# First down-projection weights in the up-projection's buffers, and another order of the loads at the turn

## The chip, the core and the metric

The kernel runs on one core of a Trainium2 chip. The metric is the device time of one execution in microseconds (us). The core has five engines that run side by side, each through its own list of instructions in order: PE (matrix products; PEld is its weight load), DVE and ACT (elementwise work), POOL, and SP, which here does nothing but issue DMA transfers. An engine that waits for one instruction holds up all that stand behind it in its list.

## The reference, cut to what matters

Two layers, 1024 tokens of 1024 channels. Each has a token mixer and then this channel mixer, about which the change is:

```python
x = layer_norm(ALPHA * x + mixed, ln1_g[l], ln1_b[l])
ff = jnp.square(jax.nn.relu(x @ w_up[l])) @ w_down[l]
x = layer_norm(ALPHA * x + ff, ln2_g[l], ln2_b[l])
```

## The kernel before

Both products of the channel mixer are done by a seven-product scheme for 2x2 blocks (Strassen's, in Winograd's form), and each float32 operand is split into a high and a low part, so that one product is three matmuls (high x high, high x low, low x high). ACT makes the high part (L97) and DVE the low one (L100).

**Up.** The hidden columns are taken in 16 pairs. A pair's weights are turned into seven forms; forms 3 to 7 stand in the tag `y4` of the pool `big` (8 buffers of 4 KB a partition). Each form is multiplied with one of seven forms of x (`x11`, `x21`, `x22`, `xt1` in the tag `b16` of `big`, the others in the up pool). Sums are in PSUM (`uz`, `uc`, `ud`); DVE and ACT make hidden parts from them (`h`), DVE the four further combinations that the down product needs (`hs`), and SP stores them to DRAM (`hd`).

**Down.** Two groups `gr` of hidden rows, in each seven products in the order 3, 1, 5, 6, 2, 7, 4, and in each product four quarters q of 24 matmuls: 96 matmuls a product. For a quarter, `down_raw` loads 2 MB of down weights (`wd`, four transfers of 512 KB) into the `b16` buffers, each as its form of x is done with; `down_forms` splits them (`wf`), loads the fitting hidden parts back (`hr`, two transfers of 256 KB) and splits these (`hf`). The sums (`db`, and `dz` for the products 1, 6, 7) are added to eight rows `yd`, loaded from DRAM into the `y4` buffers, 512 KB each. `l2g` and `l2b` are scales of the last norm, 512 KB each as written out over the partitions.

**The turn.** The pool `pd` of the down stage takes the place of the up stage's pool `pu`. A `wf` buffer can be written only when all that stood at its place is done with, the stores of `h` and `hs` to DRAM among it.

The program is written in order, and a scheduler then moves instructions past each other on each engine. All transfers named here are issued by SP, on one queue; transfer n waits for the landing of transfer n minus 8. The lines at the turn:

```python
for t in range(NTB):
    ys[t] = ytile(f"yd{l}_{t}")
for q in range(NQ):
    down_raw(0, q)
for t in range(NTB):
    nc.sync.dma_start(ys[t], xmid[l][t])
g = bcast(ln2_g[l], D, pd, "g", f"l2g{l}")
b = bcast(ln2_b[l], D, pd, "b", f"l2b{l}")
...
steps = [(gr, i) for gr in range(2) for i in PRODS]
cur = [down_forms(0, PRODS[0], q) for q in range(NQ)]
```

Of the kernel before, what the change touches and what calls it, by code (L numbers as in the profile page):

```python
# [12 lines left out]
F32R = mybir.dt.float32r  # L13
# [39 lines left out]
def encoder(ctx: ExitStack, tc: tile.TileContext, x, memt, w_f, w_v, w_mk, w_mv, w_out, w_up,  # L53
# [680 lines left out]
    for l in range(L):  # L734
# [230 lines left out]
        with ExitStack() as es:  # L965
# [18 lines left out]
            def down_forms(gr, i, q):  # L984

                r = wr[gr, q]
                v = {k: r[:, :, k[0], k[1]] for k in ((0, 0), (0, 1), (1, 0), (1, 1))}
                tt = nc.vector.tensor_tensor
                if i == 5:
                    tt(v[0, 0], v[0, 1], v[0, 0], op=ALU.subtract)  # L990
                    tt(v[0, 1], v[1, 1], v[0, 1], op=ALU.subtract)
                elif i == 6:
                    tt(v[1, 1], v[1, 1], v[0, 0], op=ALU.subtract)
                elif i == 4:
                    tt(v[1, 0], v[1, 1], v[1, 0], op=ALU.subtract)
                w = pd.tile([P, 2, 2, 512], F32R, tag="wf", name=f"wf{l}_{gr}_{i}_{q}", bufs=4)
                split(w[:, 0], w[:, 1], v[place[i]])
                hr = wts.tile([P, 2, 512], F32, tag="raw", name=f"hr{l}_{gr}_{i}_{q}", bufs=3)
                p0 = 2 * (NQ * gr + q)
                for n in range(2):  # L1000
                    loads.append(nc.sync.dma_start(hr[:, n], hd[p0 + n][:, form_of[i]]))
                if gr and i == PRODS[-1]:
                    if q % 2 == 0:
                        wr["h", q // 2] = pd.tile([P, 2, 2, 2, 512], F32R, tag="wd", name=f"hl{l}_{q}", bufs=2)
                    h = wr["h", q // 2][:, q % 2]
                else:
                    h = wts.tile([P, 2, 2, 512], F32R, tag="w8", name=f"hf{l}_{gr}_{i}_{q}", bufs=3)
                split(h[:, 0], h[:, 1], hr)
                return w, h

            for t in range(NTB):
                ys[t] = ytile(f"yd{l}_{t}")
            for q in range(NQ):
                down_raw(0, q)
            for t in range(NTB):
                nc.sync.dma_start(ys[t], xmid[l][t])
            g = bcast(ln2_g[l], D, pd, "g", f"l2g{l}")
            b = bcast(ln2_b[l], D, pd, "b", f"l2b{l}")
            touched = set()

            def add(t, j, ps, op=ALU.add):
# [24 lines left out]
            def down(ps, fm, t, start, stop):  # L1046
                w, h = fm
                ts = slice(t * P, t * P + P)
                for n in range(2):
                    for m, (a, c) in enumerate(((0, 0), (0, 1), (1, 0))):  # L1050
                        nc.tensor.matmul(ps, lhsT=h[:, a, n, ts], rhs=w[:, c, n], start=start and n == 0 and m == 0,  # L1051
                                         stop=stop and n == 1 and m == 2, skip_group_check=True)

            def done(t, spread, parts=1):
# [4 lines left out]
                    nc.sync.dma_start(dst[:, cs], ys[t][:, cs])  # L1059

            steps = [(gr, i) for gr in range(2) for i in PRODS]
            cur = [down_forms(0, PRODS[0], q) for q in range(NQ)]
            late = []
            for n, (gr, i) in enumerate(steps):
                if i in (1, 6, 7):
                    if i == 1:
                        z = banks(gr, f"dz{l}_{gr}")
                    ps = z
                else:
                    ps = banks(1 - gr, f"db{l}_{gr}_{i}")  # L1070
                nxt = []
                final = n == len(steps) - 1
                if n == 2:
                    for q in range(2):
                        down_raw(1, q)
                if final:
                    if not last:
                        first = proj_w(l + 1, FIRST)
                        xn = new_xt(f"x{l + 1}")
                    for t in range(4):  # L1080
                        for q in range(NQ):
                            down(ps[t], cur[q], t, q == 0, q == NQ - 1)
                        evict(i, t, ps[t])
                        done(t + 4, {1: 1}.get(t, 0), 2 if last and t == 3 else 1)
                        if not last:
                            to_xt(ys[t], xn, t, f"l2_{l}_{t}")
                    break
                for q in range(NQ):
                    for t in range(4):
                        down(ps[t], cur[q], t, q == 0 and i not in (6, 7), q == NQ - 1 and i not in (1, 6))  # L1090
                    if q == NQ - 1:
                        for t in range(4):
                            evict(i, t, ps[t])
                            if gr and i == 2:
                                done(t, {1: 1, 3: 1}.get(t, 0))
                    nxt.append(down_forms(*steps[n + 1], q))
                    if not gr and i == PRODS[-2] and q > 1:
                        down_raw(1, q)
                cur = nxt
# [90 lines left out]
```

## Time and profile before

| what | us |
|---|---|
| median of 3 runs | 2515.94 (2515.7 to 2519.42) |
| the profiled execution's own time | 2514.72 |
| its span, first to last instruction | 2512.9 |
| PE busy | 2335.6 |
| DVE busy | 1894.5 |
| ACT busy | 1105.5 |

The profile is of one execution. It holds each instruction's start and length by engine, what ended each idle time, the clock granted to PE as a share of full speed, and for each DMA its issue and its landing.

### The profile page before, as it was taken

What the parts mean: (1) busy time and instruction counts of PE and PEld (TensorE: products, weight loads), DVE (VectorE), ACT (ScalarE), POOL (GpSimd) and SP (SyncE); (2) the same over time, 40 slices, a digit from 0 to 9 for tenths busy, and PEclk for the clock granted to TensorE, in tenths of its full rate; (3) what the DMA queues carried; (4) which work ended last, traced back from release to release, by engine and by line L of the source; (5) the groups of instructions that cost most, each with busy time, mean ns of one, the idle gap of its engine ahead of it and who ended that gap; (6) DMA issues with size and microseconds to landing.
All of it is one profiled execution on the core that took longest, in us unless ns stands there. A gap on an engine that the chain in (4) does not pass through costs nothing.

```text
span 2512.9 us, 30298 instructions
## 1 busy us (share of the span) xinstructions
PE 2335.6 (93%) x11256; PEld 1919.2 (76%) x11256; DVE 1894.5 (75%) x2598; ACT 1105.5 (44%) x1864; POOL 486.3 (19%) x350
## 2 busy tenths in 40 slices
PE   5999989889999997999999999889989999799997
PEld 3788777677788886888878887767768888588886
DVE  7599779969756656657788977997885666476769
ACT  5212477722555543333431237874245555333332
POOL 1124176821000000000033324683100000000002
PEclk9999999999999998999999999998989999899998
DMA  9433444242344458243332336422424444934332
GB/s 317 154 125 97 152 131 127 67 147 90 114 161 148 151 213 326 92 163 98 107 109 84 116 120 187 123 69 87 168 76 153 149 155 148 385 101 159 99 92 101
DMA packets 137740, 355.74 MB, mean 142 GB/s; under 512 B 14804, under 2 KB 31956, under 8 KB 130900
## 3 DMA queue, kind: packets, MB, share of 16 engines
q1 hardware_dynamic: 137592, 353.81, 42.1%
q8 instruction: 88, 1.44, 0.3%
q14 instruction: 60, 0.49, 0.1%
HBM read 240.47 MB, written 117.47 MB: 142 GB/s over the span
## 4 chain that ended last, share of the span: by engine, by line
PE 59%; DVE 20%; issue 3%; DMA 3%; ACT 1%; SPq 0%; DVEq 0%; ACTq 0%
PE uz L873 13%; PE db L1051 12%; PE dz L1051 10%; PE uc L873 7%; PE ud L873 4%; DVE acc L344 3%; DVE s L535 3%; DVE s L557 2%; PE wo_ps L115 1%; PE wo_ps L114 1%; PE wo_ps L113 1%; DVE l_row L145 1%; PE pj L114 1%; PE pj L113 1%; PE pj L115 1%
## 5 line engine op out<-in xcount | busy, mean ns | idle before, releaser
L1051 PE MATMUL db<-wf,hf 128*128 128x512 f32 x1344 | 324.9, 403 | 22.2 <-ACT wf L97 18.6
L1051 PEld LDWEIGHTS db<-wf,hf 128*128 128x128 f32 x1344 | 258.9, 193 | 87.0 <-ACT wf L97 20.8
L163 POOL TENSOR_TENSOR yd<-yd,l2g 128x1024 f32<-128x1024 f32 x6 | 14.7, 2443 | 1345.5 <-ACT yd L162 1345.5
L1051 PE MATMUL dz<-wf,hf 128*128 128x512 f32 x1152 | 269.7, 395 | 0.0
L97 ACT ACTIVATE hf<-hr 128x1024 fp32r<-128x1024 f32 x104 | 110.3, 1061 | 353.7 <-PE db L1051 195.1
L1051 PEld LDWEIGHTS dz<-wf,hf 128*128 128x128 f32 x1152 | 217.0, 188 | 50.7
L100 DVE TENSOR_TENSOR hf<-hr,hf 128x1024 fp32r<-128x1024 f32 x104 | 127.2, 1223 | 152.4 <-ACT hf L97 152.0
L97 ACT ACTIVATE wu<-wu_r 128x512 fp32r<-128x512 f32 (+1 forms) x192 | 131.0, 699 | 227.7 <-PE uc L873 95.5
L873 PE MATMUL uz<-xt,wu 128*128 128x512 f32 x768 | 190.5, 396 | 6.0 <-ACT wu L97 6.0
L873 PE MATMUL uz<-x,wu 128*128 128x512 f32 x768 | 191.6, 396 | 0.0
L344 DVE SCALAR_TENSOR_TENSOR acc<-u,pp,acc 128x1009 f32<-128x1009 f32 (+14 forms) x120 | 182.3, 1560 | 0.6
L114 PE MATMUL pj<-x_l,wf 128*128 128x512 f32 x448 | 177.3, 396 | 2.7 <-DVE x_l L100 2.7
L113 PE MATMUL pj<-x_h,wf 128*128 128x512 f32 x448 | 178.2, 398 | 0.4 <-ACT x_h L97 0.4
L115 PE MATMUL pj<-x_h,wf 128*128 128x512 f32 x448 | 176.5, 395 | 0.0
L100 DVE TENSOR_TENSOR wu<-wu_r,wu 128x512 fp32r<-128x512 f32 (+1 forms) x192 | 145.7, 777 | 39.6 <-ACT wu L97 39.2
L873 PEld LDWEIGHTS uz<-xt,wu 128*128 128x128 f32 x768 | 144.3, 188 | 40.3 <-ACT wu L97 6.5
L537 ACT ACTIVATE s<-s,ast 128x1024 f32<-128x1024 f32 x128 | 147.2, 1151 | 55.2 <-DVE ast L535 52.9
L873 PEld LDWEIGHTS uz<-x,wu 128*128 128x128 f32 x768 | 146.4, 191 | 32.0
L890 DVE TENSOR_TENSOR h<-u,uc 128x512 f32<-128x512 f32 x64 | 44.0, 688 | 160.4 <-PE uc L873 134.2
L535 DVE CUSTOM_DVE_ANT_0 s<-sc,bt 128x1024 f32<-128x1024 f32 x128 | 153.8, 1214 | 11.6 <-PE sc L533 10.1
L100 DVE TENSOR_TENSOR wf<-wd,wf 128x1024 fp32r<-128x1024 f32 x112 | 138.1, 1236 | 26.4 <-DMA l2b<-in_ln_b 13.4
L97 ACT ACTIVATE wf<-wd 128x1024 fp32r<-128x1024 f32 x112 | 116.6, 1045 | 35.7 <-DMA hd<-hs 30.2
(261 smaller groups left out, 5375.7 us busy)
## 6 DMA issues: line engine op xcount, KB each, us to landing
hr<-hd SPq DMA_DIRECT2D x224, 256.0 KB, 2.9
wu_r<-in_w_up SPq DMA_DIRECT2D x64, 512.0 KB, 4.2
hd<-hs SPq DMA_DIRECT2D x128, 256.0 KB, 2.3
wd<-in_w_down SPq DMA_DIRECT2D x64, 512.0 KB, 7.6
hd<-h SPq DMA_DIRECT2D x96, 256.0 KB, 2.2
ks<-kd SPq DMA_DIRECT2D x32, 512.0 KB, 11.6
wf_raw<-in_w_f SPq DMA_DIRECT2D x28, 512.0 KB, 4.2
qd<-stg SPq DMA_DIRECT2D x8, 1024.0 KB, 4.2
```

What stands on the lines that cost most here:

```text
L97: nc.scalar.activation(hi, src, AF.Copy)
L100: (lo_eng or nc.vector).tensor_tensor(lo, src, f(hi), op=ALU.subtract)
L113: nc.tensor.matmul(ps, lhsT=lhs[0], rhs=rhs[0], start=start, stop=False)
L114: nc.tensor.matmul(ps, lhsT=lhs[0], rhs=rhs[1], start=False, stop=False)
L115: nc.tensor.matmul(ps, lhsT=lhs[1], rhs=rhs[0], start=False, stop=stop)
L344: nc.vector.scalar_tensor_tensor(acc[:, c, a:b], u[:, c, a + t - PAD:b + t - PAD], pp[:, k:k + 1], acc[:, c, a:b], ALU.mult, ALU.add)
L535: nc.vector.tensor_tensor_reduce(out=sc[:, m], in0=ps.rearrange("p a b -> p (a b)"), in1=bt[:, b0:b0 + T], scale=-0.125, scalar=3e38, op0= ...
L537: nc.scalar.activation(sc[:, m], sc[:, m], AF.Exp, scale=-1.0, bias=st[:, m:m + 1], accum_out=st[:, 2 + m:3 + m])
L557: nc.vector.scalar_tensor_tensor(sc[:, 0], sc[:, 1], st[:, 5:6], sc[:, 0], ALU.mult, ALU.add)
L873: nc.tensor.matmul(ps, lhsT=a[:, kc], rhs=x[:, c, kc], start=start and kc == 0 and n == 0, stop=stop and kc == 3 and n == 2, skip_group_ch ...
L890: nc.vector.tensor_tensor(h, a, ps, op=op)
L1051: nc.tensor.matmul(ps, lhsT=h[:, a, n, ts], rhs=w[:, c, n], start=start and n == 0 and m == 0, stop=stop and n == 1 and m == 2, skip_group ...
```

## The change

The first product's weight parts for q = 0 and 1 no longer take two `wf` buffers of `pd`. They take four `y4` buffers, the high and the low part each its own tile. Raw weights and forms of a quarter are written one after the other, not all raw weights first. The rows `yd` are loaded in two lots: four after q = 1, and four with the second product, into the buffers that the first weight parts leave. The norm scales are loaded with the third product, behind the raw weights of group 1.

```diff
-                w = pd.tile([P, 2, 2, 512], F32R, tag="wf", name=f"wf{l}_{gr}_{i}_{q}", bufs=4)
-                split(w[:, 0], w[:, 1], v[place[i]])
+                if not gr and i == PRODS[0] and q < 2:
+
+                    w = [big.tile([P, 2, 512], F32R, tag="y4", name=f"wf{l}_{gr}_{i}_{q}_{n}", bufs=8) for n in range(2)]
+                else:
+                    w = pd.tile([P, 2, 2, 512], F32R, tag="wf", name=f"wf{l}_{gr}_{i}_{q}", bufs=4)
+                    w = [w[:, 0], w[:, 1]]
+                split(w[0], w[1], v[place[i]])
...
-            for t in range(NTB):
-                ys[t] = ytile(f"yd{l}_{t}")
-            for q in range(NQ):
-                down_raw(0, q)
-            for t in range(NTB):
-                nc.sync.dma_start(ys[t], xmid[l][t])
-            g = bcast(ln2_g[l], D, pd, "g", f"l2g{l}")
-            b = bcast(ln2_b[l], D, pd, "b", f"l2b{l}")
+            def down_rows(ts):
+                for t in ts:
+                    ys[t] = ytile(f"yd{l}_{t}")
+                    nc.sync.dma_start(ys[t], xmid[l][t])
+
...
-                        nc.tensor.matmul(ps, lhsT=h[:, a, n, ts], rhs=w[:, c, n], start=start and n == 0 and m == 0,
+                        nc.tensor.matmul(ps, lhsT=h[:, a, n, ts], rhs=w[c][:, n], start=start and n == 0 and m == 0,
...
-            cur = [down_forms(0, PRODS[0], q) for q in range(NQ)]
+            cur = []
+            for q in range(NQ):
+                down_raw(0, q)
+                cur.append(down_forms(0, PRODS[0], q))
+                if q == 1:
+                    down_rows(range(4))
...
+                if n == 1:
+                    down_rows(range(4, NTB))
                 if n == 2:
                     for q in range(2):
                         down_raw(1, q)
+                    g = bcast(ln2_g[l], D, pd, "g", f"l2g{l}")
+                    b = bcast(ln2_b[l], D, pd, "b", f"l2b{l}")
```

What the scheduler makes of it differs from before only at the two turns from up to down, one in each layer, in the same way. On PE this stood at the turn of the first layer before (`uz_15`, `uc_15`: the last pair's sums; `db_0_3_t`: first product, token block t; `wf_0_3_q`, `hf_0_3_q`: weights and hidden parts of quarter q):

```order
L873 MATMUL uc_14_7534<-x_0_4994,wu_14_3_7381 128x512 x12
L873 MATMUL uz_15_7483<-xt_0_5338,wu_15_7_7528 128x512 x12
L873 MATMUL uc_15_7626<-x_0_4994,wu_15_3_7531 128x512 x12
L1051 MATMUL db_0_3_0_7798<-wf_0_3_0_7762,hf_0_3_0_7768 128x512
L1051 MATMUL db_0_3_1_7799<-wf_0_3_0_7762,hf_0_3_0_7768 128x512
```

and this stands there now, of which each block of `db` matmuls is shown by its first row:

```order
L873 MATMUL uc_14_7534<-x_0_4994,wu_14_3_7381 128x512 x12
L1053 MATMUL db_0_3_0_7788<-wf_0_3_0_0_7727,hf_0_3_0_7734 128x512
...
L873 MATMUL uz_15_7483<-xt_0_5338,wu_15_7_7528 128x512 x12
L1053 MATMUL db_0_3_0_7788<-wf_0_3_1_0_7742,hf_0_3_1_7749 128x512
...
L1053 MATMUL db_0_3_1_7789<-wf_0_3_0_0_7727,hf_0_3_0_7734 128x512
...
L873 MATMUL uc_15_7626<-x_0_4994,wu_15_3_7531 128x512 x12
L1053 MATMUL db_0_3_2_7790<-wf_0_3_0_0_7727,hf_0_3_0_7734 128x512
...
L1053 MATMUL db_0_3_0_7788<-wf_0_3_2_7765,hf_0_3_2_7771 128x512
L1053 MATMUL db_0_3_1_7789<-wf_0_3_2_7765,hf_0_3_2_7771 128x512
```

Matmuls of the down product now stand between the last three blocks of the up product: 6 before `uz_15`, 18 between it and `uc_15` (6 of block 0, 12 of block 1), and 24 behind it (blocks 2 and 3), before those of q = 2.

On SP the queue stood so before, from the third quarter's raw weights (`wd_0_2`) to the last store of a hidden combination but one (`hs_15_1`):

```order
L981 DMA wd_0_2_7740<-in_w_down 128x1024 x4
L1016 DMA yd_2_7724<-xmid_101 128x1024
...
L1016 DMA yd_3_7725<-xmid_101 128x1024
L1016 DMA yd_4_7726<-xmid_101 128x1024
L1016 DMA yd_5_7727<-xmid_101 128x1024
L1016 DMA yd_6_7728<-xmid_101 128x1024
...
L981 DMA wd_0_3_7745<-in_w_down 128x1024 x4
L1016 DMA yd_7_7729<-xmid_101 128x1024
L896 DMA hd_15_5209<-hs_15_2_7708 128x512
L896 DMA hd_15_5209<-hs_15_0_7706 128x512
L896 DMA hd_15_5209<-hs_15_1_7707 128x512
```

and so now:

```order
L981 DMA wd_0_2_7760<-in_w_down 128x1024 x4
...
L1019 DMA yd_0_7752<-xmid_101 128x1024
L1019 DMA yd_1_7754<-xmid_101 128x1024
L1019 DMA yd_2_7756<-xmid_101 128x1024
...
L1019 DMA yd_3_7758<-xmid_101 128x1024
L981 DMA wd_0_3_7774<-in_w_down 128x1024 x4
L896 DMA hd_15_5209<-hs_15_2_7708 128x512
L896 DMA hd_15_5209<-hs_15_0_7706 128x512
L1019 DMA yd_4_7930<-xmid_101 128x1024
L896 DMA hd_15_5209<-hs_15_1_7707 128x512
```

Four rows fewer stand ahead of `wd_0_3`, and `yd_4`, which takes a buffer of the first weight parts, now stands ahead of the store of `hs_15_1`.

On ACT the four weight parts followed the last hidden part (`h_15_3`) before; now those of q = 0 and 1 stand further up, the first of them ahead of `h_15_0`, and behind `h_15_3` stand two hidden parts and then the weights of q = 2 and 3 (DVE has the low parts in the same order):

```order
L892 ACTIVATE h_15_3_7702<-h_15_3_7702 128x512
L97 ACTIVATE hf_0_3_3_7785<-hr_0_3_3_7782 128x1024
L97 ACTIVATE hf_0_1_0_7822<-hr_0_1_0_7819 128x1024
L97 ACTIVATE wf_0_3_2_7765<-wd_0_2_7760 128x1024
L97 ACTIVATE wf_0_3_3_7779<-wd_0_3_7774 128x1024
L97 ACTIVATE wf_0_1_0_7816<-wd_0_0_7722 128x1024
```

`hf_0_3_3` and `hf_0_1_0` take the buffers of `hf_0_3_0` and `hf_0_3_1`, so they wait until PE has used these for all four token blocks. At its place in `pd`, `wf_0_3_3` now waits for the store of `hs_15_1`, as `wf_0_3_1` did before.

## Rows read from the trace of the kernel before

**Rows 1.** The page: busy time by engine, and the chain that ended last.

```profile
PE 2335.6 (93%) x11256; PEld 1919.2 (76%) x11256; DVE 1894.5 (75%) x2598; ACT 1105.5 (44%) x1864; POOL 486.3 (19%) x350
...
PE uz L873 13%; PE db L1051 12%; PE dz L1051 10%; PE uc L873 7%; PE ud L873 4%; DVE acc L344 3%; DVE s L535 3%; DVE s L557 2%; PE wo_ps L115 1%; PE wo_ps L114 1%; PE wo_ps L113 1%; DVE l_row L145 1%; PE pj L114 1%; PE pj L113 1%; PE pj L115 1%
```

**Rows 2.** Timeline of PE at the first turn: start, length, what, [idle before, releaser].

```profile
943.73 2.96 PE L873 MATMUL uz<-xt,wu 128*128 128x512 f32 x12
949.38 4.61 PE L873 MATMUL uc<-x,wu 128*128 128x512 f32 x12 [2.69 <-DVE h L890]
957.03 2.03 PE L1051 MATMUL db<-wf,hf 128*128 128x512 f32 x4 [3.05 <-ACT wf L97]
960.00 6.70 PE L1051 MATMUL db<-wf,hf 128*128 128x512 f32 x20 [0.94 <-DVE wf L100]
973.03 0.79 PE L1051 MATMUL db<-wf,hf 128*128 128x512 f32 x1 [6.32 <-ACT wf L97]
974.29 18.27 PE L1051 MATMUL db<-wf,hf 128*128 128x512 f32 x71 [0.47 <-DVE wf L100]
992.39 3.89 PE L1051 MATMUL dz<-wf,hf 128*128 128x512 f32 x16
```

**Rows 3.** Timeline of PE at the second turn.

```profile
2158.27 2.96 PE L873 MATMUL uz<-xt,wu 128*128 128x512 f32 x12
2163.92 4.17 PE L873 MATMUL uc<-x,wu 128*128 128x512 f32 x12 [2.69 <-DVE h L890]
...
2207.12 3.18 PE L1051 MATMUL dz<-wf,hf 128*128 128x512 f32 x13
```

**Rows 4.** The chain that ended last, in order of time: start, length, what.

```profile
955.80 6.84 DMA hd<-h
962.70 8.99 DMA hd<-hs
...
992.56 22.31 PE dz L1051 x96
...
2150.75 7.56 DMA wd<-in_w_down
```

**Rows 5.** Windows: length, busy PE, PEld, DVE, ACT, POOL; granted clock, DMA share, GB/s.

```profile
560.00:566.00 6.00, 3.49 (x23) 2.90 (x24) 5.96 (x6) 1.09 (x2) 0.77 (x1) 1.00 0.42 170
566.00:572.00 6.00, 6.00 (x28) 4.95 (x27) 5.86 (x13) 2.30 (x5) 0.00 (x0) 1.00 0.61 201
...
950.00:955.00 5.00, 3.98 (x11) 2.67 (x9) 0.69 (x1) 1.92 (x4) 0.00 (x0) 0.66 1.05 416
...
990.00:1010.00 20.00, 20.00 (x88) 16.22 (x87) 17.72 (x17) 6.70 (x7) 0.00 (x0) 1.00 0.33 108
...
935.00:940.00 5.00, 5.00 (x23) 4.06 (x22) 1.29 (x2) 2.87 (x5) 0.00 (x0) 1.00 1.04 415
```

**Rows 6.** Timeline of ACT and SP at the first turn.

```profile
961.53 2.27 SPq L896 DMA_DIRECT2D hd<-hs  x4
...
971.92 2.95 ACT L97 ACTIVATE wf<-wd 128x1024 fp32r<-128x1024 f32 x3 [14.94 <-DMA hd<-hs]
```

**Rows 7.** `wd`: issue to landing, the four transfers issued from 924.62 on.

```profile
DMA to landing us min/median/max: 4.6/5.5/7.0
```

**Rows 8.** `wd`: issue to landing, the one transfer issued at 934.95.

```profile
DMA to landing us min/median/max: 7.6/7.6/7.6
```

**Rows 9.** The page's groups: work, out<-in, count | busy, mean ns of one | idle before.

```profile
L97 ACT ACTIVATE hf<-hr 128x1024 fp32r<-128x1024 f32 x104 | 110.3, 1061 | 353.7 <-PE db L1051 195.1
...
L100 DVE TENSOR_TENSOR hf<-hr,hf 128x1024 fp32r<-128x1024 f32 x104 | 127.2, 1223 | 152.4 <-ACT hf L97 152.0
...
L890 DVE TENSOR_TENSOR h<-u,uc 128x512 f32<-128x512 f32 x64 | 44.0, 688 | 160.4 <-PE uc L873 134.2
```

**Rows 10.** Timeline of DVE behind the first turn.

```profile
973.01 3.50 DVE L100 TENSOR_TENSOR wf<-wd,wf 128x1024 fp32r<-128x1024 f32 x3 [13.06 <-ACT wf L97]
...
992.12 1.88 DVE L1027 SCALAR_TENSOR_TENSOR yd<-yd,db 128x512 f32<-128x512 f32 x3
```

**Rows 11.** Timeline of PE, an idle time elsewhere.

```profile
561.90 1.09 PE L780 MATMUL x<-ident,y 128*128 128x128 f32 x8 [2.04 <-DVE y L170]
```

## The prediction

> **What bounds the kernel now.** I read the page first. PE is busy 93% of the span, and the chain that ended last runs mostly through the matmuls of the channel mixer [rows 1]. The change touches only the two turns from up to down, so what matters is what PE waits for there. The timeline of PE shows it [rows 2]. Between the last `uz` block, which begins at 943.73, and the first `dz` matmul, at 992.39, stand 120 matmuls: 12 `uz`, 12 `uc`, 96 `db`. A block of 96 takes 22.31 us where nothing disturbs it [rows 4], so one matmul costs 0.2324 us and 120 cost 27.9. They took 992.39 - 943.73 = 48.66. So 20.8 us are lost. At the second turn the stretch is 2207.12 - 2158.27 = 48.85 us [rows 3], and 21.0 are lost. Both together are 41.7 us, and no change to these turns can give back more.
>
> Where do the 20.8 go? The idle times in brackets are 2.69 + 3.05 + 0.94 + 6.32 + 0.47 = 13.5 us [rows 2]. The other 7.3 are matmuls at half speed behind each idle time: the 12 of `uc` took 4.61 us behind the wait of 2.69, against 2.96 for the 12 of `uz`, and the granted clock from 950 to 955 is a mean of 0.66, between its two levels, 2.4 and 1.2 GHz [rows 2, 5].
>
> What do the waits end on? ACT stands idle for 14.94 us until a store of `hs` has landed, and then makes three weight parts at once [rows 6]. The chain runs the same way: a store of `h` (6.84 us), a store of `hs` behind it in the queue (8.99), then PE [rows 4]. A store alone is not that slow; the queue is full. Before and during the turn it moves 415 GB/s, its share over 1, and behind the turn 108 GB/s [rows 5]. So PE waits at the turn for the queue, and the first weight parts wait for stores only because their buffers lie in `pd`.
>
> **The change part by part.** No instruction of any size is added or removed; DVE, ACT and the queue get the same work. I follow the first turn through the lists of the change, in trace time.
>
> *First quarters.* The parts of q = 0 and 1 now wait for raw weights and for `y4` buffers. The last transfer of the raw weights of q = 1, issued at 934.95, landed 7.6 us later, at 942.5 [rows 8]. One row load `yd_0` stood ahead of it and is gone. 512 KB are 0.524 MB, at 415 GB/s 1.26 us [rows 5], so it lands at 941.3. ACT needs 1.05 us and DVE 1.2 [rows 9], so both parts are there at 943.7.
>
> *PE runs on.* The new order on PE then has work without a gap, at 0.2324 us each: 6 `db` from 943.7 to 945.1, `uz` to 947.9, 6 of q = 1 (ready since 943.7) to 949.3, block 1 to 952.1, `uc` to 954.9, blocks 2 and 3 to 960.5. Before `uc` PE had waited 2.69 us for an eviction by DVE [rows 2]; now 18 matmuls, 4.2 us, cover that wait. Were this cover gone, the 2.7 us and the slow clock behind them would be back. Block 3 needs the last eviction of `uc` (0.69 us of DVE [rows 9]), and block 2 covers it with 2.8 us.
>
> *Third quarter.* Here a stall is left. ACT makes `hf_0_3_3` and `hf_0_1_0` ahead of the weights of q = 2, and `hf_0_1_0` takes a buffer that PE uses until 960.5. So ACT has it at 961.8 and the high part of the weights at 962.8; DVE, behind its own `hf_0_1_0`, has the low part at 964.2 (1.06 and 1.22 us each [rows 9]). PE waits 2.4 us, does the 4 matmuls that need only the high part, waits 0.5, and is through q = 2 at 968.95.
>
> *Fourth quarter.* `wf_0_3_3` waits for the store of `hs_15_1`. That store is now queued behind `yd_4`, which SP can issue only when PE has used the first weight parts, at 959.1. Ahead of both in the queue are `yd_3` and `wd_0_3`, issued when `uc` is through, at 954.9. A load that finds the queue nearly empty lands after 4.6 us [rows 7], so `yd_3` lands at 959.7. Behind it come four raw weights, two stores of half the size, `yd_4` and the store itself: 5 x 1.26 + 3 x 0.63 = 8.2 us, so it lands at 967.9. ACT has the high part at 969.1, DVE the low one at 970.4. PE waits 0.3 and 1.0 us and ends the product at 970.45 + 23 x 0.2324 = 975.8, against 992.39.
>
> The Trainium skill, DMA: Bandwidth & Descriptors, section Where 436 GB/s comes from, says that between HBM and SBUF the HBM side binds, at about 358 GB/s for a core. This trace does not agree, with 415 in a whole stretch [rows 5]. By the page's figure the 8.2 us would be an estimated 9.5 and the store 1.3 us later, some 2.6 us for the kernel.
>
> *The clock.* The idle time left at the first turn is 2.4 + 0.5 + 0.3 + 1.0 = 4.2 us. Does the clock fall behind it? The trace has no idle time of 2.4 us, so I bound it. Behind 2.04 us elsewhere [rows 11] the granted clock stayed at 1.00 in both windows [rows 5]: nothing. Behind 3.05 + 0.94, 20 matmuls took 6.70 us where they need 4.8: 1.9 [rows 2]. Behind 2.69 alone the cost was 4.61 - 2.96 = 1.65 at the first turn and 4.17 - 2.96 = 1.2 at the second [rows 2, 3]. 2.4 with 0.5 after it lies nearer to 2.69, so I take 1.4 a turn and keep 0 and 1.9 as bounds.
>
> *What is late next.* The second product begins 16 us earlier, with DVE less far ahead. From `wf_0_3_3` to the hidden part that the third product needs first, DVE has 22 large operations at 1.17 us and 4 evictions at 0.63 [rows 10]: 28.2 us from 969.2, so 997.4. PE asks for it at 975.8 + 22.3 = 998.1. It fits by 0.7 us, so I cost it at nothing; if the operations ran at the 1.22 of [rows 9] it would cost 0.4 us a turn. The 2 MB of `yd_4` to `yd_7`, the raw weights of group 1 and the scales come later but are asked for a whole product later or more; the queue is nearly idle there, 108 GB/s [rows 5], and that covers them.
>
> *Second turn.* The list is the same. The last raw weight of q = 1 was issued at 2150.75 and landed 7.56 us later [rows 4], at 2158.3, 1.3 us later against the matmuls than at the first turn. The cover at the first turn was 947.9 - 943.7 = 4.2 us, so it holds here too.
>
> *The sum.* Lost before 41.7. Left: 2 x (4.2 + 1.4) = 11.2. Gain 30.5 us. The profiled execution took 2514.72, with 1.8 us outside its span of 2512.9; it lies 1.2 under the median of the runs, 2515.94. Behind the first product of each layer's down stage the lists are those of before, so the gain goes to the end: 2515.94 - 30.5 = 2485.5, 1.2% less.
>
> **The rivals.** *Smoother:* the store of `hs_15_1` lands earlier and the clock does not fall. For it: 2.04 us did not bring the clock down. Against it: the order on ACT and DVE forces the 2.9 us at q = 2 whatever the queue does. At 2.9 a turn 5.8 is left, which gives 2480.
>
> *Queue or DVE late:* the store lands as late against its issue as before, 9 us or more [rows 4], and DVE, 17.7 of 20 us busy behind the turn [rows 5], becomes the bound of the second and third product. Against it: the queue has fewer bytes ahead of the store now. 2 to 5 us a turn: 2490 to 2496.
>
> *Hidden anyway:* the first product ends when it did before, since the last raw weights can be loaded only when the up stage is through. Against it: before, they were issued at 957 and nothing but ACT's wait for the store kept them from use. No change: 2516.
>
> *Slower:* down matmuls now stand in PE's list ahead of the last up blocks, and weight parts in ACT's and DVE's list ahead of the last hidden parts. If the raw weights of q = 1 land late, the up stage itself stops, with its stores, and everything behind. Each us beyond the cover of 4.2 costs 1 us; the gain of 15 a turn is used up at 19 us later than worked out. Transfers took 4.6 to 7.6 us in [rows 7, 8], so this needs a queue three times as slow; at 24 us late it would be 2525.
>
> That the change does nothing is ruled out by the lists: the blocks did move on PE.
>
> **How the numbers follow.** Forecast 0.47, smoother 0.15, late 0.28, hidden 0.05, slower 0.05. What this kernel's measurement can tell from no change is about 0.2%, 5 us. The first three are all faster by more: 0.90; same 0.05; slower 0.05. The range goes from 2477, the smoother case with 3 of its 5.8 us gone as well, to 2496, the far end of the late case; about 0.15 lies outside. The forecast's own range is 2481 to 2489, from the bounds of the clock and 1 us a turn either way for the landing.
>
> **What would show it.** Right: on PE no wait between `uz_15` and block 3, the clock at 1.00 up to 960; then a wait of 2 to 3 us ended by ACT's or DVE's weights of q = 2, a smaller one at q = 3; the first `dz` matmul near 976 to 978, 15 us earlier, and the same at the second turn. ACT's wait for a store of `hs` falls from 14.94 us to under 6. Wrong: waits of PE at `uz_15` or `uc_15` for weight parts (the slower case), a wait in the second or third product for `hf` by DVE, or a clock that stays down longer.

## The result and the profile after

The changed kernel takes 2484.24 us (median of 4 runs, 2482.02 to 2487.55) where the kernel before took 2516.16 in the same session: 0.9872 of it, with an interval of 0.9856 to 0.9888. In a later session it was 2485.05 against 2515.51, 0.9881 (0.9865 to 0.9898). The forecast was 2485.5. The profiled execution took 2482.02, with a span of 2480.2, so again 1.8 us lie outside the span.

The timeline of PE at the first turn, with start, length, what, and in brackets the idle time before and what ended it; it answers to [rows 2]:

```profile
943.28 1.52 PE L1053 MATMUL db<-wf,hf 128*128 128x512 f32 x6
944.64 2.96 PE L873 MATMUL uz<-xt,wu 128*128 128x512 f32 x12
947.43 4.26 PE L1053 MATMUL db<-wf,hf 128*128 128x512 f32 x18
951.53 2.88 PE L873 MATMUL uc<-x,wu 128*128 128x512 f32 x12
954.25 5.60 PE L1053 MATMUL db<-wf,hf 128*128 128x512 f32 x24
961.94 1.20 PE L1053 MATMUL db<-wf,hf 128*128 128x512 f32 x4 [2.09 <-ACT wf L97]
963.39 6.46 PE L1053 MATMUL db<-wf,hf 128*128 128x512 f32 x20 [0.26 <-DVE wf L100]
970.66 0.50 PE L1053 MATMUL db<-wf,hf 128*128 128x512 f32 x1 [0.81 <-ACT wf L97]
971.92 5.61 PE L1053 MATMUL db<-wf,hf 128*128 128x512 f32 x23 [0.76 <-DVE wf L100]
977.37 22.47 PE L1053 MATMUL dz<-wf,hf 128*128 128x512 f32 x96
999.68 22.48 PE L1053 MATMUL db<-wf,hf 128*128 128x512 f32 x96
```

The waits of 2.69 and 3.05 us are gone: `uc` begins right behind 18 down matmuls. The same 120 matmuls now take 977.37 - 943.28 = 34.09 us in place of 48.66. Since they need 27.9, 6.2 us are still lost: 2.09 + 0.26 + 0.81 + 0.76 = 3.92 idle, and 2.3 in matmuls that take longer. Some 1.6 of the 2.3 are the low clock (20 matmuls take 6.46 us, against 4.91 at the full clock in the kernel with the buffers alone, below). The rest is at the starts behind idle times: the one matmul at 970.66 takes 0.50 us, and not 0.23, at the full clock. The second and third product (`dz`, then `db`) show no wait.

The timeline of PE at the second turn, for [rows 3]:

```profile
2141.18 1.52 PE L1053 MATMUL db<-wf,hf 128*128 128x512 f32 x6
...
2159.84 1.20 PE L1053 MATMUL db<-wf,hf 128*128 128x512 f32 x4 [2.09 <-ACT wf L97]
2161.28 6.92 PE L1053 MATMUL db<-wf,hf 128*128 128x512 f32 x21 [0.25 <-DVE wf L100]
2168.97 5.62 PE L1053 MATMUL db<-wf,hf 128*128 128x512 f32 x23 [0.76 <-DVE wf L100]
2174.43 22.47 PE L1053 MATMUL dz<-wf,hf 128*128 128x512 f32 x96
```

Here the stretch is 2174.43 - 2141.18 = 33.25 us in place of 48.85; 5.35 are lost, 3.10 of them idle. The two turns gave back 14.57 + 15.60 = 30.2 us. The spans of the two profiles differ by 2512.9 - 2480.2 = 32.7; of the other 2.5 us, 0.45 stand ahead of the first turn and 2.1 between the first product of the first turn and the second turn. That second stretch (1163.8 us in this profile) is 1165.0 us in the later profile of the changed kernel, and the four runs spread over 5.5 us, so they are not shown to come from the change.

ACT at the first turn, the last row answering to [rows 6]:

```profile
958.53 1.06 ACT L97 ACTIVATE hf<-hr 128x1024 fp32r<-128x1024 f32 x1 [2.06 <-PE db L1053]
959.89 1.06 ACT L97 ACTIVATE hf<-hr 128x1024 fp32r<-128x1024 f32 x1 [0.30 <-PE db L1053]
960.85 1.04 ACT L97 ACTIVATE wf<-wd 128x1024 fp32r<-128x1024 f32 x1
969.55 2.96 ACT L97 ACTIVATE wf<-wd 128x1024 fp32r<-128x1024 f32 x3 [7.66 <-DMA hd<-hs]
```

The first three rows are the stall at q = 2: ACT waits for PE's release of the `hf` buffers, makes two hidden parts, and only then `wf_0_3_2`. The fourth is q = 3: ACT still waits for a store of `hs`, 7.66 us in place of 14.94.

Windows of the first turn, in the columns of [rows 5]:

```profile
950.00:960.00 10.00, 9.85 (x44) 7.83 (x42) 3.74 (x6) 4.10 (x7) 0.00 (x0) 1.00 1.03 397
963.70:967.05 3.35, 3.35 (x9) 2.61 (x8) 0.00 (x0) 0.00 (x0) 0.00 (x0) 0.50 1.04 413
967.10:977.40 10.30, 8.73 (x37) 6.54 (x36) 6.76 (x6) 4.85 (x5) 0.00 (x0) 1.00 1.03 415
980.00:1000.00 20.00, 20.00 (x88) 16.23 (x87) 20.00 (x20) 6.27 (x7) 0.00 (x0) 1.00 0.72 272
```

The granted clock is 1.00 (2.4 GHz) while PE runs on, 0.50 (1.2 GHz) from 963.70 to 967.05, behind the wait at q = 2, and 1.00 again. The queue stays full to the end of the first product. Behind the turn DVE is busy 20.00 of 20 us, yet PE waits for nothing: what was costed at nothing there did cost nothing.

### The profile page after: what moved, and what is told of

It is laid out like the page before. It is cut to its first block, busy times and chain, and to the rows that moved or that the text cites. A ratio compares the mean times of both kernels' runs of the same rounds, so it can differ in the third digit from the quotient of the medians.

```text
span 2480.2 us, 30322 instructions
## 1 busy us (share of the span) xinstructions
PE 2321.3 (94%) x11256; PEld 1908.5 (77%) x11256; DVE 1893.9 (76%) x2598; ACT 1105.8 (45%) x1864; POOL 485.0 (20%) x350
## 4 chain that ended last, share of the span: by engine, by line
PE 64%; DVE 27%; issue 4%; DMA 4%; ACT 2%; SPq 0%; DVEq 0%; ACTq 0%
PE uz L873 14%; PE db L1053 12%; PE dz L1053 10%; DVE acc L344 7%; PE uc L873 7%; PE ud L873 4%; DVE s L535 3%; DVE s L557 3%; PE pj L113 2%; PE pj L114 2%; PE pj L115 2%; DVE ast L556 1%; PE wo_ps L115 1%; DVE at L100 1%; PE wo_ps L114 1%
## 5 line engine op out<-in xcount | busy, mean ns | idle before, releaser
L1053 PE MATMUL db<-wf,hf 128*128 128x512 f32 x1344 | 319.6, 398 | 7.0 <-ACT wf L97 5.0
L100 DVE TENSOR_TENSOR wf<-wd,wf 128x1024 fp32r<-128x1024 f32 x112 | 138.0, 1235 | 26.2 <-ACT wf L97 19.2
L532 PE MATMUL sc<-ks,qs 128*128 128x512 f32 x256 | 111.8, 437 | 21.3 <-DVE ast L535 21.1
```

Of the source, the lines that this page charges most:

```text
L100: (lo_eng or nc.vector).tensor_tensor(lo, src, f(hi), op=ALU.subtract)
L532: nc.tensor.matmul(ps[:, hf], lhsT=qs[:, m, q], rhs=ks[:, 2 * m, cs], start=True, stop=False)
L1053: nc.tensor.matmul(ps, lhsT=h[:, a, n, ts], rhs=w[c][:, n], start=start and n == 0 and m == 0, stop=stop and n == 1 and m == 2, skip_group ...
```

## The experiments

They ask three things: which part of the change gives the gain, whether the scales are worth nothing, as the prediction had it, and what sets the 5 to 6 us a turn that are left.

### The order of the loads alone, and the scales alone

```diff
-                if not gr and i == PRODS[0] and q < 2:
+                if False:
```

> The loads keep the new order, but the weight parts of q = 0 and 1 go back to their old buffers in pd. On PE, ACT and DVE this gives the lists of the kernel before; only the queue's order is new. Theory (the parts waited for stores because of their buffers, and the 48 down matmuls among the last up blocks are what fills PE's waits): no gain beyond noise, 2510 to 2520 us, ACT again idle for 12 us or more ahead of the first weight parts on a store of hs, and 48 us or more from the uz_15 block to the first dz matmul. Rival (the queue's order relieves the stores, and that is the gain): 2490 us or less, ACT's wait under 8 us.

Measured: 2518.01 us against 2516.62, a ratio of 1.0007 (0.9997 to 1.0017). PE in this kernel:

```profile
946.81 4.57 PE L873 MATMUL uc<-x,wu 128*128 128x512 f32 x12 [2.69 <-DVE h L890]
954.43 1.83 PE L1053 MATMUL db<-wf,hf 128*128 128x512 f32 x4 [3.05 <-ACT wf L97]
...
971.78 0.80 PE L1053 MATMUL db<-wf,hf 128*128 128x512 f32 x1 [7.57 <-ACT wf L97]
```

Every wait of [rows 2] is back, to the hundredth for the first two, and ACT is idle for 16.29 us until a store of `hs` has landed. The queue's order by itself gives nothing. (Ahead of `wd_0_3` stand seven rows in the kernel before and four in the changed one, three fewer and not four.)

The other half of the new order, the scales, moved alone in the kernel before:

```diff
-            g = bcast(ln2_g[l], D, pd, "g", f"l2g{l}")
-            b = bcast(ln2_b[l], D, pd, "b", f"l2b{l}")
...
                 if n == 2:
                     for q in range(2):
                         down_raw(1, q)
+                    g = bcast(ln2_g[l], D, pd, "g", f"l2g{l}")
+                    b = bcast(ln2_b[l], D, pd, "b", f"l2b{l}")
```

> The kernel before, with only the scale loads moved to the third product, so that the four weight parts in pd lie 8 KB earlier in each partition: q = 1 then waits for the store of hs_15_3 in place of hs_15_1, and q = 2 for hs_15_0 in place of hs_15_3. Theory (place in pd decides which store is waited for): the first wait for weight parts ends later by the landing of two more stores, 1 to 2 us a turn, some of it taken back at q = 2, so 2516 to 2522 us. Rival (two loads less ahead of the stores in the queue speed the stores up): 2512 us or less.

Measured: 2518.21 us against 2517.46, 0.9997 (0.9986 to 1.0008). The move alone gives nothing; the small loss that the theory gave can't be told from none.

### The buffers alone

```diff
+            down_rows(range(4))
             for q in range(NQ):
                 down_raw(0, q)
                 cur.append(down_forms(0, PRODS[0], q))
-                if q == 1:
-                    down_rows(range(4))
```

> The parts of q = 0 and 1 go to the y4 buffers as in the changed kernel, but the first four row loads are written ahead of all raw weights again, which puts yd_0 ahead of the raw weights of q = 1, yd_1 and yd_2 ahead of those of q = 2, and two rows in place of one ahead of the store of hs_15_1. Theory: the buffers carry the gain; a row load ahead costs 1.26 us of queue where it stands in front of what PE waits for, so 0 to 3 us a turn, 2484 to 2490 us. Rival (buffers and order are needed together, since the raw weights of q = 1 come too late without the order): the up stage waits at its last block, and half the gain or more is gone, 2500 us or more.

Measured: 2491.08 us against 2516.62, 0.9894 (0.9878 to 0.9911); the profiled execution, 2498.12, is the longest of its four. PE in it:

```profile
949.90 2.88 PE L873 MATMUL uc<-x,wu 128*128 128x512 f32 x12
...
962.58 1.20 PE L1053 MATMUL db<-wf,hf 128*128 128x512 f32 x4 [2.09 <-ACT wf L97]
964.03 4.91 PE L1053 MATMUL db<-wf,hf 128*128 128x512 f32 x20 [0.26 <-DVE wf L100]
975.23 0.80 PE L1053 MATMUL db<-wf,hf 128*128 128x512 f32 x1 [6.29 <-ACT wf L97]
```

The last `uc` block has no wait ahead of it, since down matmuls stand there: the buffers carry 25.5 of the 32 us, and the rival falls. What is missing stands at q = 3, 6.29 us of wait in place of 0.81 (in the longest execution, so less than that in the others). Three things are mixed in it: two rows stand ahead of the last stores, the parts of q = 3 lie where `hs_15_3` stood, the last of the four stores, and the engines' lists change too (PE has 14 down matmuls between `uz_15` and `uc_15` and 34 behind, none before). So the remaining 6 us are not shown to be the order of the rows. The upper end of the theory, 2490, was a little low.

### The scales first, and their place without their loading

```diff
+            g = bcast(ln2_g[l], D, pd, "g", f"l2g{l}")
+            b = bcast(ln2_b[l], D, pd, "b", f"l2b{l}")
             cur = []
...
-                    g = bcast(ln2_g[l], D, pd, "g", f"l2g{l}")
-                    b = bcast(ln2_b[l], D, pd, "b", f"l2b{l}")
```

> The changed kernel with the norm scales loaded and allocated ahead of the down stage's loads, as before; PE, ACT and DVE keep the lists of the changed kernel, and on the queue only the two scale loads change places with the raw weights of group 1. Theory: they were costed at nothing, since the queue is nearly empty there, so the same time as the changed kernel within 0.1%, 2481 to 2488 us. Rival (the 1 MB of scales holds up the loads of the second product): 2 us or more a turn, 2488 us or more, with waits of PE in the second or third product.

Measured: 2491.63 us against 2516.62, 0.9902 (0.9887 to 0.9916). The theory, nothing, fell; yet PE has none of the waits in the second or third product that the rival wanted. The wait that grew is that at q = 3, from 0.81 to 2.43 us at the first turn. The reason lies in `pd`: with the scales allocated first, every `wf` lies 8 KB further on in each partition, and `wf_0_3_3` comes to stand where `hs_15_3` stood in `pu`, no longer where `hs_15_1` stood. To tell the place from the two loads, the scales are allocated first and loaded where the changed kernel loads them:

```diff
+            g, b = [pd.tile([P, D], F32, tag=tag, name=f"l2{tag}{l}", bufs=1) for tag in "gb"]
             cur = []
...
-                    g = bcast(ln2_g[l], D, pd, "g", f"l2g{l}")
-                    b = bcast(ln2_b[l], D, pd, "b", f"l2b{l}")
+                    for to, src in ((g, ln2_g[l]), (b, ln2_b[l])):
+                        nc.sync.dma_start(to, src[None, :].to_broadcast([P, D]))
```

> The changed kernel with nothing but the place of the two scales in pd altered: they are allocated first, and loaded where the changed kernel loads them. All engines and the queue keep the changed kernel's lists; only the parts of q = 3 now lie where hs_15_3 stood, in place of hs_15_1, as in the run with the scales first. Theory (what the scales cost there was the place, not their loading): ACT waits for the store of hs_15_3, PE's wait at q = 3 is 2.4 to 2.8 us in place of 0.8, the first dz matmul 3 us or more later in each turn, 2490 to 2493 us. Rival (it was the two loads in the queue): the time of the changed kernel, 2484 us.

Measured: 2489.3 us against 2517.71, 0.9895 (0.9877 to 0.9913). PE's wait at q = 3 was 1.50 and 1.57 us, less than the theory's 2.4. Since this interval touches that of the changed kernel, both were run again side by side.

> The changed kernel once more, on the same chip as the next run. Theory: 2482 to 2487 us; ACT waits for the store of hs_15_1, and PE's wait for ACT at q = 3 is under 1 us in both turns. Rival (its first profile was a lucky one, and the landing varies more than the place matters): waits of 1.5 us or more at q = 3 here too, and a time within 2 us of the next run's.

> The changed kernel with the scales allocated first in pd and nothing else altered, beside the changed kernel on one chip. Theory (the place alone, by the store that it makes q = 3 wait for): PE's wait for ACT at q = 3 is 1.5 us or more in both turns, and the time 3 to 7 us above the run before it. Rival (the place is worth nothing that can be told): within 2 us of it.

Measured: 2485.05 us (0.9865 to 0.9898 of before) and 2491.39 (0.9888 to 0.9918), a difference of 6.3 us. PE in the changed kernel, from the low parts of q = 2 on, with no wait for ACT at q = 3:

```profile
963.06 6.83 PE L1053 MATMUL db<-wf,hf 128*128 128x512 f32 x21 [0.24 <-DVE wf L100]
970.65 5.61 PE L1053 MATMUL db<-wf,hf 128*128 128x512 f32 x23 [0.76 <-DVE wf L100]
```

and with the scales' place alone altered, from q = 3 on:

```profile
971.76 0.50 PE L1053 MATMUL db<-wf,hf 128*128 128x512 f32 x1 [1.84 <-ACT wf L97]
973.02 7.15 PE L1053 MATMUL db<-wf,hf 128*128 128x512 f32 x23 [0.76 <-DVE wf L100]
```

with this window, and the issue to landing of the last store, issued at 962.24:

```profile
973.90:977.30 3.40, 3.40 (x10) 2.63 (x9) 3.40 (x4) 1.60 (x2) 0.00 (x0) 0.50 1.03 422
```

```profile
DMA to landing us min/median/max: 8.3/8.3/8.3
```

All lists, the queue's among them, are the same in both kernels; only addresses differ. The last of the four stores lands at 970.5, and ACT starts at 970.65, 27.3 us behind the first `db`. In the changed kernel it starts on the landing of the store before that, 25.3 us behind the first `db` (968.28). The price has two parts: the wait of 1.84 us, and a second stretch at the low clock behind it, in which the same 23 matmuls take 7.15 us in place of 5.61. Together 3.4 a turn. The second part does not always come: in the earlier run of this kernel, behind 1.50 + 0.77 us at the first turn, the 23 took 5.62 us, and behind 1.57 + 0.77 at the second, 7.15. The place of the scales is worth some 6 us of the gain. The two loads themselves are not shown to cost anything: 2491.63 with them, 2489.3 and 2491.39 without.

### What sets the rest: ACT's order or the store

```diff
-                split(h[:, 0], h[:, 1], hr)
+                if not gr and ((i == PRODS[0] and q == 3) or (i == PRODS[1] and q == 0)):
+                    with tc.issue_after(wr["third"][0].ins), tc.issue_after(wr["third"][1].ins):
+                        split(h[:, 0], h[:, 1], hr)
+                else:
+                    split(h[:, 0], h[:, 1], hr)
```

`wr["third"]` holds the two instructions that make the weights of q = 2.

> The changed kernel with hf_0_3_3 and hf_0_1_0 held behind the weight parts of q = 2 on ACT and DVE. That takes away the stall of 2.1 us at q = 2, but hf_0_3_3 now stands behind wf_0_3_3, which waits for the store of hs_15_1. Theory (what is left of the loss is set by the landing of that store, and the stall at q = 2 only takes some of the same wait): the wait moves from q = 2 to q = 3, the first dz matmul comes 0 to 3 us later than in the changed kernel, 2484 to 2490 us. Rival (the order on ACT and DVE sets the rest, as the prediction has it): PE gains 2 us a turn and more with the clock, 2480 us or less.

Measured: 2489.26 us against 2516.62, 0.9889 (0.9874 to 0.9904). PE and ACT:

```profile
953.24 11.19 PE L1060 MATMUL db<-wf,hf 128*128 128x512 f32 x48
969.70 1.22 PE L1060 MATMUL db<-wf,hf 128*128 128x512 f32 x2 [5.28 <-ACT hf L98]
```

```profile
967.64 1.06 ACT L98 ACTIVATE wf<-wd 128x1024 fp32r<-128x1024 f32 x1 [11.24 <-DMA hd<-hs]
```

PE runs 48 matmuls through q = 2 without a wait, and then waits 5.28 us at q = 3 for a hidden part that stands behind `wf_0_3_3`, and so behind the store. The stall at q = 2 went and the time did not fall: in this order the store's landing sets the end of the product. The reverse edit leaves the lists of ACT and PE, and DVE's up to the end of the first product, and takes one row from ahead of the store:

```diff
-                nc.sync.dma_start(hd[p][:, i], h)
+                kept.append(nc.sync.dma_start(hd[p][:, i], h))
...
                 if n == 1:
-                    down_rows(range(4, NTB))
+                    with tc.issue_after(kept[-1].ins):
+                        down_rows(range(4, NTB))
```

> The changed kernel with the rows yd_4 to yd_7 held behind the last stores of hs, so that none stands ahead of the store of hs_15_1. ACT, DVE and PE keep their lists. Theory (q = 3 waits for this store, and one row ahead of it costs 1.26 us of queue): the store lands 1 to 2 us earlier, PE's wait of 0.81 us at q = 3 for ACT is gone, and the first dz matmul comes 0.8 to 1.3 us earlier in each turn, 2481 to 2484 us. Rival (the row is free, since DVE makes hs_15_1 too late for it to matter): PE's waits stay as in the changed kernel, 2484 us.

Measured: 2481.51 us (2480.62 to 2482.32) against 2517.71, 0.9853 (0.984 to 0.9867). PE:

```profile
944.06 1.52 PE L1055 MATMUL db<-wf,hf 128*128 128x512 f32 x6
...
962.73 1.20 PE L1055 MATMUL db<-wf,hf 128*128 128x512 f32 x4 [2.10 <-ACT wf L97]
964.17 12.35 PE L1055 MATMUL db<-wf,hf 128*128 128x512 f32 x44 [0.25 <-DVE wf L100]
976.36 22.47 PE L1055 MATMUL dz<-wf,hf 128*128 128x512 f32 x96
```

ACT starts the parts of q = 3 at 968.54, 24.5 us behind the first `db`, where it was 26.3 in the changed kernel's first profile:

```profile
968.54 2.96 ACT L97 ACTIVATE wf<-wd 128x1024 fp32r<-128x1024 f32 x3 [5.87 <-DMA hd<-hs]
```

No wait is left at q = 3. The turns take 976.36 - 944.06 = 32.30 and 31.99 us, 1.8 and 1.3 less than in the changed kernel's first profile, 0.8 and 0.7 less than in its second (33.15 and 32.71). So one row of 512 KB ahead of the store was worth about what PE waited for it. Now the stall at q = 2 is what is left.

### Without the store, and what comes then

```diff
-                if not gr and i == PRODS[0] and q < 2:
+                if not gr and i == PRODS[0] and q != 2:
...
-                if q == 1:
-                    down_rows(range(4))
+            down_rows(range(2))
...
                     if q == NQ - 1:
+                        if n == 0:
+                            down_rows(range(2, 4))
```

> The changed kernel with the parts of q = 3 in y4 buffers too, so that no first weight part but q = 2 lies in pd; rows yd_0 and yd_1 come behind all raw weights, the others later. ACT then makes the parts of q = 3 ahead of those of q = 2, as soon as the raw weights land. Theory (with the store out of the way, the raw weights' landing sets q = 3): ACT waits for no store of hs; but q = 2 now stands behind that landing, at about 965, so PE waits some 7 us at q = 2 and none at q = 3; 24 matmuls of the second product stand ahead in PE's list, and the sum is -1 to +3 us a turn against the changed kernel, 2482 to 2490 us. Rival (rows late): the evictions of the first product wait for yd, PE waits in the second or third product, 2492 us or more.

Measured: 2489.79 us against 2517.71, 0.9889 (0.9875 to 0.9902), at the theory's upper end. PE waits 4.90 us at q = 2 and not at q = 3. Only 2 matmuls of the second product stand ahead in the list, not the 24 that the expectation counted on. A weight part early in the wrong order is no help. With the order mended (the parts of q = 3 held behind those of q = 2, and `hf_0_3_3` and `hf_0_1_0` behind both of q = 2):

```diff
+                if not gr and i == PRODS[0] and q == 3:
+                    with tc.issue_after(wr["third"][0].ins), tc.issue_after(wr["third"][1].ins):
+                        parts = split(w[0], w[1], v[place[i]])
```

> The parts of q = 3 in y4 buffers, and on ACT and DVE the parts of q = 2 first, those of q = 3 next, then hf_0_3_3 and hf_0_1_0: neither a store of hs nor a hidden part stands ahead of a weight part. Theory: no wait at q = 2; q = 3 starts when its raw weights have landed, about 965, and ACT and DVE have made them and hf_0_3_3, so PE waits 2 to 3 us there, and the first dz matmul comes 2.5 to 4 us earlier than in the changed kernel in each turn, 2475 to 2480 us. Rival (rows and hidden rows, now behind one another in the queue, come late): PE waits in the second or third product for hf or for an eviction, and the time is 2484 us or more.

Measured: 2483.68 us against 2517.71, 0.986 (0.9847 to 0.9874). PE:

```profile
943.94 1.52 PE L1064 MATMUL db<-wf,hf 128*128 128x512 f32 x6
...
967.10 5.28 PE L1064 MATMUL db<-wf,hf 128*128 128x512 f32 x22 [0.52 <-DVE hf L101]
972.21 12.29 PE L1064 MATMUL dz<-wf,hf 128*128 128x512 f32 x52
987.29 10.60 PE L1064 MATMUL dz<-wf,hf 128*128 128x512 f32 x44 [2.79 <-DVE hf L101]
```

The first product is all but free of waits: its stretch, from the first `db` at 943.94, is 28.3 us where 27.9 are needed. But 2.79 us come back in the second product, where PE waits for a hidden part by DVE, and the time stays above the theory's 2475 to 2480. Was it late because its rows came late in the queue? The next kernel puts them first (the row loads of the kernel before it, `down_rows(range(2))` and the later lot, are taken out):

```diff
+                    if n == 0:
+                        wr["hid"] = loads[-1]
+                    if n == 0 and q == 2:
+                        with tc.issue_after(loads[-1].ins):
+                            down_rows(range(4))
...
+                    with tc.issue_after(wr["hid"].ins):
                         for q in range(2):
                             down_raw(1, q)
```

> The kernel with the parts of q = 3 in y4 buffers and the weights of q = 2 and 3 first, and now the hidden rows hr_0_1_2 ahead of the first row loads in the queue, and the raw weights of group 1 behind the hidden rows hr_0_1_3. In the run before it PE waited 2.8 us in the second product of each turn, ended by DVE's hf, whose rows had stood behind five raw weights and rows. Theory (that wait was queue position alone): it is gone, the start of the third product comes 2 to 3 us earlier in each turn than there, and 4 to 5.5 us earlier than in the changed kernel, 2474 to 2479 us. Rival (DVE or the rows become the bound of the second product, since everything moved up): waits of the same size for DVE or an eviction, 2481 to 2485 us.

Measured: 2481.17 us (2478.8 to 2484.0) against 2517.46, 0.9856 (0.9841 to 0.987). PE:

```profile
986.36 10.53 PE L1064 MATMUL dz<-wf,hf 128*128 128x512 f32 x44 [1.71 <-DVE hf L101]
998.77 24.13 PE L1064 MATMUL db<-wf,hf 128*128 128x512 f32 x96 [1.89 <-ACT hf L98]
```

and ACT, with the part of `hf_0_1_2` that PE waits for, and a window of the same kernel:

```profile
974.30 1.06 ACT L98 ACTIVATE hf<-hr 128x1024 fp32r<-128x1024 f32 x1 [1.66 <-DMA hr<-hd]
...
997.66 1.06 ACT L98 ACTIVATE hf<-hr 128x1024 fp32r<-128x1024 f32 x1 [5.23 <-DMA hr<-hd]
```

```profile
968.60:986.30 17.70, 16.04 (x70) 12.70 (x68) 17.70 (x19) 8.17 (x9) 0.00 (x0) 1.00 1.01 399
```

The theory fell. The rows now land early enough: ACT has its part at 975.4, 11 us ahead of the end of the wait at 986.36. DVE has not come to it: it was busy for all of the window, with weight forms, evictions and low parts. With the first product ended at 972, DVE is the bound of the second, as the rival said. Whether by its load or by the order of its list is open: seven of the operations that DVE did ahead of this low part make weight forms for the third and fourth product (L991, L992, L994), and no kernel here puts them behind it. The wait of 1.89 us is for ACT, which at 997.66 has waited for the hidden rows of the third product. They stand behind the raw weights of group 1, as in the changed kernel, and these were held back here. At the second turn PE waits 0.19 us there, for DVE. This kernel and that with the rows behind the store are the fastest, some 3 us under the changed kernel; their intervals still overlap its interval, so that the times alone don't settle it.

## Why the prediction was right, point by point

- **Bound of the gain.** 41.7 us lost at the two turns, and nothing else touched: the turns gave back 30.2 of them, against 30.5 forecast.
- **First quarters and PE without a gap.** Worked out for 943.7 to 960.5. Measured: the first `db` at 943.28, and no wait until 959.85, the end of the last block ahead of q = 2. ACT began the parts of q = 1 at 941.68, on the landing of their raw weights, for which 941.3 was worked out.
- **Third quarter.** 2.4 + 0.5 worked out, 2.09 + 0.26 measured, at both turns, in every kernel that keeps this order on ACT.
- **Fourth quarter.** The landing of the store was mis-sized. Worked out: 967.9, or 24.2 us behind the first `db`; measured: 969.5, 26.2 behind it. The rows are the landing of `yd_3`, issued at 954.44, that of the store, issued at 960.46, and what the queue moved between the two landings:

```profile
DMA to landing us min/median/max: 6.0/6.0/6.0
```

```profile
DMA to landing us min/median/max: 9.0/9.0/9.0
```

```profile
DMA packets 1250, 3.53 MB, mean 390 GB/s; under 512 B 138, under 2 KB 138, under 8 KB 1249
```

  Two terms made it late: `yd_3` took 6.0 us and not the 4.6 of a queue nearly empty, and from its landing at 960.4 to that of the store at 969.5 passed 9.0 us and not 8.2, at a mean of 390 GB/s and not 415. PE's two waits were 0.81 + 0.76 and, at the second turn, 0 + 0.76, against 0.3 + 1.0. So PE waited for the parts of q = 3 even after the stretch at the low clock, and the store set the end of the product: 975.8 - 943.7 = 32.1 us worked out without the clock, 34.1 measured, later by the same 2.0 us as the store. On the Trainium skill's DMA: Bandwidth & Descriptors, section Where 436 GB/s comes from, the windows above (397 to 415 GB/s) again do not agree with its 358 for a core; the 9.0 us lie between the 8.2 of the trace's rate and the estimated 9.5 of the page's.
- **Clock.** 1.4 us a turn taken, with bounds 0 and 1.9. Measured in the same way, 20 matmuls took 6.46 us at the first turn and 4.91 at the full clock elsewhere; at the second turn 21 took 6.92, where some 5.14 would do. That is 1.6 and 1.8, inside the bounds. But the sum adds this cost to the waits at q = 3, and at these turns it ran while the store was still on its way, and, since PE still waited behind it, lengthened nothing. The kernel with the rows behind the store shows it: there ACT starts 24.5 us behind the first `db`, PE does not wait at q = 3, and with the low clock 4.4 and 4.1 us are lost at the two turns, not 5.6. The prediction's 7.3 us "at half speed" in the kernel before hold the slow starts too: five of them at 0.50 - 0.23 us are an estimated 1.3.
- **The sum left** was to be 11.2 us; it is 6.2 + 5.35 = 11.55. That it came so near is luck in part: the store, later than worked out by 2.0 us at the first turn, took the place of the 1.4 us for the clock, which the sum should not have added there.
- **DVE's margin** at the third product was worked out at 0.7 us. Measured: from 970.64 to 998.10 for the same 22 operations and 4 evictions, 27.5 us and not 28.2, and PE comes to the third product at 999.68, so 1.6 us and no wait:

```profile
996.88 1.22 DVE L100 TENSOR_TENSOR hf<-hr,hf 128x1024 fp32r<-128x1024 f32 x1
```

  That it is thin was shown by the kernel that ends the first product 5 us earlier: there DVE is waited for, in the second product. The queue, taken as nearly idle here at 108 GB/s, moved 272 from 980 to 1000, and PE waited for none of it.
- **The scales** were costed at nothing, and their loading is not shown to cost anything. But moving them is worth some 6 us by the place that it gives `wf_0_3_3`. The forecast had this in it unseen, since it followed the changed kernel's own lists, in which q = 3 waits for `hs_15_1`. As an account of which edit does what, that sentence of the prediction was wrong.
- **The rivals.** *Hidden anyway* and *slower* fell with the first timeline. Of *late*, the first half came about: the store landed 9.0 us behind its issue, and ACT's wait for it was 7.66 us, more than the "under 6" set. Of that, 0.81 + 0.76 us at most showed as waits of PE at q = 3. The second half, DVE as the bound, did not. *Smoother* failed on both counts: the store landed later, not earlier, and the clock fell. The place from which *slower* would decide, raw weights of q = 1 late by more than the cover, was not tried in a kernel that leaves the order on PE as it is.

## What to carry to other kernels

Where one stage's pool takes the place of another's, each buffer waits for whatever stood at its own address, so the order in which tiles are allocated decides which store the next stage waits for, even with every list of instructions unchanged. The first operands of a stage belong in buffers that PE alone releases, and the matmuls that they feed then fill the waits of the stage before. When a wait goes, look for the next one before mending it: here the store, the order on ACT and DVE stood one behind the other, each with a wait of about 1 to 3 us a turn.

## What the runs showed of the hardware

- The length of a wait does not tell whether the clock falls. Behind 2.04 us it stayed at 1.00 [rows 11]. Behind the same 2.09 + 0.26 us, 20 matmuls took 6.46 us in the changed kernel, with the clock at 0.50 for part of them, and 4.91 in the kernel with the buffers alone, where it stayed at 1.00 (from 963.90 to 969.00). Behind the same 2.69 us, 12 matmuls took 4.57 us at the first turn of the kernel with the order alone, and 3.00 at its second:

```profile
2164.94 3.00 PE L873 MATMUL uc<-x,wu 128*128 128x512 f32 x12 [2.69 <-DVE h L890]
```

  Behind the 2.79 us of the kernel with q = 3 in `y4` it stayed there too:

```profile
987.30:990.80 3.50, 3.50 (x15) 2.88 (x16) 3.50 (x4) 0.91 (x1) 0.00 (x0) 1.00 1.02 420
```

- The same store behind the same list landed at different times: in two profiles of the changed kernel ACT started 26.3 and 25.3 us behind the first `db` (969.55 - 943.28, and 968.28 - 942.95). What tells the price of the place in `pd` is therefore the pair of kernels run side by side, not one profile of each.
